# Interleaving the groups at a change of pass, in a Strassen-Winograd feed-forward stage

## The chip, the cores and the metric

The kernel runs on one core of one Trainium2 chip. The metric is the device time of one execution in microseconds (us), as the median of the runs. An engine works through its own queue of instructions in order; TensorE (PE) multiplies, VectorE (DVE) and ScalarE (ACT) work element by element, GpSimd (POOL) does a few sums, SyncE (SP) issues the DMAs.

## What is computed

One layer of a hybrid decoder on 512 positions of width 2048, in float32. The part that matters here is the last one, the convolutional GLU, with 5632 hidden channels:

```
h = rms_norm(x, norm2_w)
u = causal_dwconv(h @ w_up, ffn_conv_w, ffn_conv_b)   # w_up: 2048 x 11264, conv over 3 positions
u_gate, u_val = jnp.split(u, 2, axis=-1)
return x + (jax.nn.silu(u_gate) * u_val) @ w_down     # w_down: 5632 x 2048
```

Ahead of it stand the combined input projection, the attention heads, the state-space heads and the output projection.

## The kernel before

Both large products of the feed-forward stage are done by the Strassen-Winograd scheme: a block product of 2 x 2 blocks takes seven block products, P1 to P7, and no longer eight. Each product multiplies a sum of weight blocks by a sum of activation blocks; the latter is called a *kind*. There are seven kinds, one for each product: P5 uses KT1, P1 K11, P6 KT2, P2 K21, P7 KT3, P3 K22, P4 KT4. To keep float32 accuracy on fp32r matmuls, every operand is split into a high part (an ACT copy to fp32r) and a low part (a DVE subtraction), and a product is high x high, high x low and low x high: 24 matmuls of 128 x 256 where there are 8 blocks of contraction, 21 where there are 7.

A *group* is one set of seven products. There are 44 groups of the up stage (0 to 43; NF is 44), one for each 128 gate and 128 value channels, and then three *passes* of the down stage over 7, 8 and 7 blocks of hidden channels (PASSES), eight groups each: 44 to 51, 52 to 59, 60 to 67. In the text, 43.P7 is product P7 of group 43. Within the up stage the kinds stay; every pass has kinds of its own, made from what the up stage stored in DRAM (gd). b_load reads half a kind into a buffer ld (three deep in the first transition, five later), b_split makes its high part on ACT (L1151) and its low part on DVE (L1152) into the tile cmb of this kind. A kind's tile is one buffer, so that the next pass's version can be written only after the last product that uses the old one. That change of kinds is called a transition here.

A product accumulates in a tile x (one PSUM bank, two halves of 256 columns, two buffers) or y (P2). After a product its half is read out: up_after copies P1, P6 and P5 to cP tiles on ACT (L1241) and adds P2, P7, P3 and P4 on DVE (L1243 to L1249); down_after copies or adds into acc (L1219 on ACT, L1221 on DVE). After P4 of an up group follows its tail on DVE: the norm factor, two convolutions, the gate (up_side, L1259 to L1282) and, every second group, sums of the result (L890 to L893).

All order is by hand. The list items holds the products as TensorE takes them, pos the place of each. For product number k the function step_slot(k) issues: what events holds for k (weight loads, some sums), the low part of operand k+2 (split_lo, L1103), what after holds for k (sums s1 and s3, tails, kind splits), the high part of operand k+3 (split, L1094). Weight sums are s1, s2 and s4 on DVE (L1073, L1076 and L1081, L1083) and s3 on POOL (L1069). Weight loads come from SP (L1062), with four buffers rawa and two rawb.

The order of the products before is that of one loop, the same for all groups: a group's P5, P1, P6, P2, P7 with the P3 and P4 of the group ahead between them.

```
for gi in range(1, len(groups) + 1):
    for d, x in ((0, "P5"), (1, "P3"), (0, "P1"), (1, "P4"), (0, "P6"), (0, "P2"), (0, "P7")):
        put(gi - d, x)
```

Of the kernel before, what the change touches and what calls it, by code (L numbers as in the profile page):

```python
# [33 lines left out]
NF = FF // 128  # L34
# [153 lines left out]
def body(ctx, tc, xT, wi, wz, wo, wu, wd0, wd1, wd2, pp, pf, outT, dbg={}):  # L188
# [99 lines left out]
    def pc(name, i=0, n=1):  # L288
        o = _PC[name] + i
        return (p2["par"] if name[0] == "f" else par)[:, o:o + n]  # L290
# [511 lines left out]
    for half in range(2):  # L802
        box = {}
# [154 lines left out]
    for i in range(4, NK):  # L958
        box = {}
# [65 lines left out]
    def side_tile(pool, shape, name, bufs=1):  # L1025
        return pool.tile([128] + shape, F32, name=name, bufs=bufs)


    groups = []
# [10 lines left out]
    items, pos = [], {}  # L1040

    def put(gi, *names):
        for x in names:
            if 0 <= gi < len(groups):
                pos[gi, x] = len(items)
                items.append((gi, x))

    put(0, "P1", "P5", "P2", "P6", "P7")
    for gi in range(1, len(groups) + 1):
        for d, x in ((0, "P5"), (1, "P3"), (0, "P1"), (1, "P4"), (0, "P6"), (0, "P2"), (0, "P7")):  # L1050
            put(gi - d, x)


    raw, chain, parts = {}, {0: pre_op["s"]}, {0: pre_op["P1"]}
    cols = lambda gi: groups[gi]["n"] * 128
# [31 lines left out]
    def split(k):  # L1087
        if k >= len(items):
            return
        gi, x = items[k]  # L1090
        n = cols(gi)
        src = raw[gi, SOURCE[x]] if x in SOURCE else chain[gi]
        h = lp.tile([128, 1024], F32R, name="hi2", bufs=3)
        se.activation(h[:, :n], src[:, :n], AF.Copy)  # L1094
        parts[k] = (h, src)
# [11 lines left out]
    events, after = {}, {}  # L1107

    def at(slot, fn, *args, where=events):
        where.setdefault(slot, []).append(lambda: fn(*args))  # L1110

    for gi in range(len(groups)):
        p5, p1 = pos[gi, "P5"], pos[gi, "P1"]
        p6 = pos[gi, "P6"]
        at(pos[gi, "P4"] - 6, load, gi, "22b")
        if gi:
            at(p5 - 8, load, gi, "21"), at(p5 - 8, load, gi, "22")
            at(p1 - 7, load, gi, "11"), at(pos[gi, "P2"] - 7, load, gi, "12")
        if gi:
            at(p5 - 3 if gi > 1 else 1, add, gi, "s1", where=after)  # L1120
            at(p5 - 3 if gi > 1 else 7, add, gi, "s3", where=after)
        else:
            at(0, add, gi, "s3", where=after)
        at(max(p5 - 1, p6 - 4) if gi else -1, add, gi, "s2"), at(pos[gi, "P3"] - 3, add, gi, "s4")
# [35 lines left out]

    for p in range(len(PASSES)):
        g0 = NF + 8 * p
        base = pos[g0 - 1, "P5"]
        slots = [2, 4, 5, 7, 8, 9, 9, 10, 11, 11, 12, 13, 14, 15]
        k0 = len(b_list)
        b_list += [(p, t, h) for t in (KT1, K11, KT2, K21, KT3, K22, KT4) for h in range(2)]
        early = 5
        for q in range(14):
            at(base + slots[q], b_split, k0 + q, where=after)
        for q in range(14):  # L1170
            at(base - 6 + q // 2 if q < early else base + slots[q - (5 if p else 3)] + 1, b_load, k0 + q)
        if p == 0:
            at(base + 36, down_pool, where=after)

    def twin(kinds, n):

# [29 lines left out]
    box = {}  # L1206
# [29 lines left out]
    def up_after(g, x):  # L1236
        X, i = g["X"], g["i"]
        ug, uv = box["ug%d" % (i % 2)], box["uv%d" % (i % 2)]
        if x in ("P1", "P6", "P5"):
            g[x] = side_tile(box["pool"], [256], "c" + x, 2 if x == "P5" else 1)  # L1240
            se.activation(g[x], X[:, 256:] if x == "P5" else X[:, :256], AF.Copy)  # L1241
        elif x == "P2":
            ve.tensor_tensor(ug[:, 2:258], g["Y"][:, :256], g["P1"], op=OP.add)  # L1243
        elif x == "P7":
            ve.tensor_tensor(uv[:, 258:514], X[:, :256], g["P5"], op=OP.add)
        elif x == "P3":
            ve.tensor_tensor(ug[:, 258:514], X[:, 256:], g["P6"], op=OP.add)
        else:
            ve.tensor_tensor(uv[:, 2:258], X[:, :256], rbc[:, :256], op=OP.mult)  # L1249
            up_side(i, ug, uv)  # L1250

    def up_side(i, ug, uv):
        pool = box["pool"]
        tt = {}

        def conv(u, ci, name, n):
            if n == 0:
                tt[name] = side_tile(pool, [S], name)
                se.activation(tt[name], u[:, 2:514], AF.Identity, bias=pc("fcb", ci), scale=pc("fcw", ci * 3 + 2))  # L1259
            ve.scalar_tensor_tensor(tt[name], u[:, n:n + S], pc("fcw", ci * 3 + n), tt[name],  # L1260
                                    op0=OP.mult, op1=OP.add)

        def val0():
            conv(uv, NF + i, "tv", 0)
            se.activation(tt["tg"], tt["tg"], AF.Silu)

        def last():
            if i % 2 == 0:
                box["gt"] = side_tile(pool, [8, 256], "gt")
            o = 2 * (i % 2)  # L1270
            ve.tensor_tensor(box["gt"][:, o:o + 2, :].rearrange("p a b -> p (a b)"), tt["tg"], tt["tv"], op=OP.mult)

        def t_sums(n):
            sums(ve, box["gt"], n)
            if n:
                pr = i // 2
                p = max(q for q in range(3) if PASSES[q][0] <= pr)
                at(t0 + (11 if i < NF - 1 else 10), sy.dma_start, gd[p][:, pr - PASSES[p][0]], box["gt"])

        t0 = pos[i, "P4"] + (15 if i >= NF - 2 else 0)  # L1280
        for d, fn in ((0, lambda: ve.tensor_tensor(ug[:, 2:514], ug[:, 2:514], rbc, op=OP.mult)),
                      (1, lambda: ve.tensor_tensor(uv[:, 258:514], uv[:, 258:514], rbc[:, 256:], op=OP.mult)),  # L1282
                      (3, lambda: conv(ug, i, "tg", 0)), (4, lambda: conv(ug, i, "tg", 1)), (5, val0),
                      (6, lambda: conv(uv, NF + i, "tv", 1)), (6, last)):
            at(t0 + d, fn, where=after)
        if i % 2:
            at(t0 + 7, t_sums, 0, where=after), at(t0 + (10 if i < NF - 1 else 8), t_sums, 1, where=after)
# [13 lines left out]
    for gi, g in enumerate(groups):  # L1301
        if g["ph"] == "down":
            p5 = pos[gi, "P5"]
# [20 lines left out]
    def run(slot, where=events):  # L1324
        for fn in where.pop(slot, ()):
            fn()

    def step_slot(slot):
        run(slot)
        if slot > 1:  # L1330
            split_lo(slot + 2)
        run(slot, after)
        if slot > 0:
            split(slot + 3)

    for n in range(2):
# [22 lines left out]
    split_lo(3)  # L1359
    next(last)  # L1360
    at(2, lambda: list(last), where=after)
    for k, (gi, x) in enumerate(items):
        g = groups[gi]
        if x == "P5" and gi or k == 0:
            g["X"] = box["ps"].tile([128, 512], F32, name="x")
        if x == "P2":
            g["Y"] = box["ps"].tile([128, 512], F32, name="y")
        out = g["Y"][:, :256] if x == "P2" else g["X"][:, 256:] if x in ("P5", "P3") else g["X"][:, :256]
        h, l = parts.pop(k)
        bk = g["kinds"][KIND[x]]  # L1370
        n = g["n"]
        fresh = x in ("P5", "P2") if k > 1 else k == 0
        if x == "P3" and (gi in (1, 2, 4, 15, 30) or gi >= NF and g["m"] in (1, 2, 4)):
            tw = box["twin"]
            for a, b, last in ((h, bk[:, 1], False), (h, tw, False), (l, tw, True)):
                for q in range(n):
                    pe.matmul(out, a[:, q * 128:(q + 1) * 128], b[:, q, :], start=False,  # L1377
                              stop=last and q == n - 1, skip_group_check=True)
            (up_after if g["ph"] == "up" else down_after)(g, x)
            step_slot(k)  # L1380
            continue
        for part in ((range(n - 1), range(n - 1, n)) if k < 4 else (range(n),)):
            for q in part:
                w = h[:, q * 128:(q + 1) * 128]
                pe.matmul(out, w, bk[:, 0, q, :], start=fresh and q == 0, stop=False, skip_group_check=True)  # L1385
                pe.matmul(out, w, bk[:, 1, q, :], start=False, stop=False, skip_group_check=True)  # L1386
            for q in part:
                pe.matmul(out, l[:, q * 128:(q + 1) * 128], bk[:, 0, q, :], start=False, stop=q == n - 1,  # L1388
                          skip_group_check=True)
        if k == 0:  # L1390
            continue
        if k == 1:
            start_up()
            up_after(g, "P1")
            step_slot(0)
        (up_after if g["ph"] == "up" else down_after)(g, x)
        step_slot(k)
    for slot in sorted(events):
        run(slot)
# [21 lines left out]
```

## Time and profile before

| | us |
|---|---|
| median of 3 runs (2064.23 to 2066.41) | 2065.65 |
| the profiled execution | 2066.1 |
| its span, first to last instruction | 2064.1 |
| TensorE busy | 2041.0 |
| VectorE busy | 1556.5 |
| ScalarE busy | 1018.4 |

The feed-forward stage begins at about 780 us in the span. The up stage runs to about 1617, the three passes follow. Lines of the profile name the tile written and the tiles read (out<-in), then shape, count, busy time and, in brackets, the idle time ahead of the instruction with what ended it.

### The profile page before, as it was taken

Reading aid. Unit: us, or ns where it says so; the run is one execution under the profiler, and the core shown is the slowest. Engines: PE = TensorE matmul, PEld = TensorE weight load, DVE = VectorE, ACT = ScalarE, POOL = GpSimd, SP = SyncE. Lnnn points to the kernel's source line nnn. Section 1 sums busy time; section 2 is a strip of 40 time slices with the busy share of each in tenths; the row PEclk is TensorE's granted clock in tenths of the full one; section 3 lists DMA queues with packets and bytes.
Section 4 is the critical chain, followed back from the end, with each engine's and each line's share of the span. In section 5 each row is a group of like instructions: output and inputs, shape, how many; then the busy total and the mean of one; then the engine's idle time right before and its main releaser. Section 6 shows DMA issues by size and latency. Waiting matters only on the chain.

```text
span 2064.1 us, 37659 instructions
## 1 busy us (share of the span) xinstructions
PE 2041.0 (99%) x15366; PEld 1929.7 (93%) x15366; DVE 1556.5 (75%) x2185; ACT 1018.4 (49%) x1513; POOL 221.9 (11%) x127
## 2 busy tenths in 40 slices
PE   9999999999999999999999999999999999999999
PEld 8889888888888889999999999999999899999999
DVE  6535555345565558999999999999999987967876
ACT  6433435344444446555555555555555654644643
POOL 0020000000000001101110110111111111211210
PEclk9999999999999999999999999999999999999999
DMA  5232222332224546445445444444446667856873
GB/s 196 79 109 92 82 72 72 102 103 83 82 72 134 177 160 227 158 149 195 154 152 186 164 160 168 174 164 158 171 177 205 217 187 213 263 154 206 256 227 122
DMA packets 111228, 320.84 MB, mean 155 GB/s; under 512 B 10384, under 2 KB 34768, under 8 KB 108240
## 3 DMA queue, kind: packets, MB, share of 16 engines
q1 hardware_dynamic: 108320, 308.48, 44.2%
q0 software_dynamic: 2736, 9.96, 3.0%
q8 instruction: 120, 1.97, 0.4%
q14 instruction: 52, 0.43, 0.1%
HBM read 276.43 MB, written 43.55 MB: 155 GB/s over the span
## 4 chain that ended last, share of the span: by engine, by line
PE 94%; DVE 3%; DMA 1%; issue 1%; ACT 1%; SPq 0%; POOL 0%; DVEq 0%; ACTq 0%; POOLq 0%
PE acc L183 31%; PE x L1386 16%; PE x L1388 16%; PE x L1385 16%; PE sm L183 4%; PE y L1386 3%; PE y L1388 3%; PE y L1385 3%; PE x L1377 2%; DVE cmb L1152 1%; DVE lo L1103 1%; DMA ld<-gd 0%; DMA rawa<-wu 0%; DVE lo L183 0%; DMA raw<-wi 0%
## 5 line engine op out<-in xcount | busy, mean ns | idle before, releaser
L1386 PE MATMUL x<-cmb,hi 128*128 128x256 f32 x3054 | 715.7, 277 | 8.6 <-DVE cmb L1152 8.6
L1385 PE MATMUL x<-cmb,hi 128*128 128x256 f32 x3054 | 715.2, 277 | 2.8 <-ACT cP L1241 1.5
L1386 PEld LDWEIGHTS x<-cmb,hi 128*128 128x128 f32 x3054 | 574.1, 188 | 10.7 <-DVE cmb L1152 10.5
L1385 PEld LDWEIGHTS x<-cmb,hi 128*128 128x128 f32 x3054 | 574.1, 188 | 3.6 <-issue 1.8
L1388 PE MATMUL x<-cmb,lo 128*128 128x256 f32 x3054 | 411.9, 277 | 0.3 <-DVE lo L1103 0.3
L1388 PEld LDWEIGHTS x<-cmb,lo 128*128 128x128 f32 x3054 | 376.8, 188 | 0.5 <-DVE lo L1103 0.5
L183 DVE TENSOR_TENSOR lo<-raw,hi 128x512 fp32r<-128x512 f32 (+1 forms) x240 | 164.4, 691 | 229.1 <-ACT hi L183 212.3
L1094 ACT ACTIVATE hi<-s 128x1024 fp32r<-128x1024 f32 (+1 forms) x201 | 200.9, 1000 | 214.4 <-DVE s L1073 142.9
L183 PE MATMUL acc<-A,hi 128*128 128x512 f32 x704 | 279.2, 397 | 0.9 <-ACT hi L183 0.9
L183 PE MATMUL acc<-A,lo 128*128 128x512 f32 x704 | 275.5, 391 | 0.0
L183 PE MATMUL acc<-B,hi 128*128 128x512 f32 x704 | 274.9, 390 | 0.0
L183 ACT ACTIVATE hi<-raw 128x512 fp32r<-128x512 f32 (+1 forms) x240 | 150.0, 629 | 238.2 <-PE acc L183 202.0
L1103 DVE TENSOR_TENSOR lo<-s,hi 128x1024 fp32r<-128x1024 f32 (+1 forms) x201 | 238.3, 1186 | 29.1 <-issue 26.0
L1069 POOL TENSOR_TENSOR rawb<-rawa,rawb 128x1024 f32<-128x1024 f32 (+1 forms) x67 | 166.4, 2484 | 833.7 <-DVE s L1073 816.2
L1103 DVE TENSOR_TENSOR lo<-rawa,hi 128x1024 fp32r<-128x1024 f32 (+1 forms) x203 | 240.4, 1184 | 18.7 <-PE x L1388 12.8
L1094 ACT ACTIVATE hi<-rawa 128x1024 fp32r<-128x1024 f32 (+1 forms) x203 | 208.5, 1027 | 12.1 <-PE x L1386 10.5
L183 PEld LDWEIGHTS acc<-A,lo 128*128 128x128 f32 x704 | 132.5, 188 | 28.7 <-DVE lo L183 0.6
L183 PEld LDWEIGHTS acc<-A,hi 128*128 128x128 f32 x704 | 132.9, 189 | 27.0 <-ACT hi L183 1.2
L183 PEld LDWEIGHTS acc<-B,hi 128*128 128x128 f32 x704 | 132.8, 189 | 26.1
L1241 ACT ACTIVATE cP<-x 128x256 f32<-128x256 f32 x132 | 50.6, 384 | 197.7 <-PE x L1388 197.7
L183 PE MATMUL acc<-hi,A 128*128 128x256 f32 (+2 forms) x448 | 134.6, 300 | 0.7 <-DVE u L183 0.7
L183 PE MATMUL acc<-hi,B 128*128 128x256 f32 (+2 forms) x448 | 132.7, 296 | 0.0
(236 smaller groups left out, 2895.2 us busy)
## 6 DMA issues: line engine op xcount, KB each, us to landing
rawa<-wu SPq DMA_DIRECT2D x175, 512.0 KB, 3.6
raw<-wi SPq DMA_DIRECT2D x79, 512.0 KB, 3.6
rawa<-wd SPq DMA_DIRECT2D x64, 448.0 KB, 4.3
rawb<-wu SPq DMA_DIRECT2D x44, 512.0 KB, 4.5
gd<-gt SPq DMA_DIRECT2D x22, 1024.0 KB, 4.4
raw<-wo SPq DMA_DIRECT2D x32, 512.0 KB, 3.6
rawa<-wd SPq DMA_DIRECT2D x32, 512.0 KB, 4.3
ld<-gd SPq DMA_DIRECT2D x27, 512.0 KB, 6.9
```

The lines of the kernel that those rows point to most:

```text
L183: return fn(out, *args, **kw)
L1069: (po if gi else ve).tensor_tensor(r, raw[gi, "11"][:, :n], r, op=OP.subtract)
L1094: se.activation(h[:, :n], src[:, :n], AF.Copy)
L1103: ve.tensor_tensor(l[:, :n], src[:, :n], h[:, :n].bitcast(F32), op=OP.subtract)
L1152: ve.tensor_tensor(lo, ld[:, :m, :], hi.bitcast(F32), op=OP.subtract)
L1241: se.activation(g[x], X[:, 256:] if x == "P5" else X[:, :256], AF.Copy)
L1377: pe.matmul(out, a[:, q * 128:(q + 1) * 128], b[:, q, :], start=False, stop=last and q == n - 1, skip_group_check=True)
L1385: pe.matmul(out, w, bk[:, 0, q, :], start=fresh and q == 0, stop=False, skip_group_check=True)
L1386: pe.matmul(out, w, bk[:, 1, q, :], start=False, stop=False, skip_group_check=True)
L1388: pe.matmul(out, l[:, q * 128:(q + 1) * 128], bk[:, 0, q, :], start=False, stop=q == n - 1, skip_group_check=True)
```

## The change

For six pairs of groups, (42, 43), (44, 45), (50, 51), (52, 53), (58, 59) and (60, 61), the products are put in pairs. The second group's product follows the first group's of the same name from P2 on, and in the pairs behind a transition from P5 on. In the pairs ahead of a transition, the P3 and P4 of the group before are still to be done; they go between the first group's P5, P1 and P6, and the second group's P5, P1 and P6 follow in a row. A group that stands behind two pairs (46, 54, 62) has no older P3 and P4 left to put between its own products. The 14 half kinds of a pass are split at slots 7 to 25, counted from the P5 of the last pair, where they were split at slots 2 to 15, counted from the P5 of the last group. The weight loads near the transitions are called two products later. The tails of groups 42 and 43 start 15 and 21 products after their P4. Ahead of the up stage's second group, the high part of operand 5 goes behind the read-out of 0.P6 on ACT. cP1 and cP6 have two buffers.

```diff
+    PAIRS = {NF - 2, NF, NF + 6, NF + 8, NF + 14, NF + 16}
     put(0, "P1", "P5", "P2", "P6", "P7")
-    for gi in range(1, len(groups) + 1):
-        for d, x in ((0, "P5"), (1, "P3"), (0, "P1"), (1, "P4"), (0, "P6"), (0, "P2"), (0, "P7")):
-            put(gi - d, x)
-
+    gi, open_ = 1, 0
+    while gi < len(groups):
+        c, d = gi, gi + 1
+        if gi not in PAIRS:
+            put(c, "P5")
+            if open_ is not None:
+                put(open_, "P3")
+            put(c, "P1")
+            if open_ is not None:
+                put(open_, "P4")
+            put(c, "P6", "P2", "P7")
+            open_ = c
+            gi += 1
+            continue
+        if open_ is None:
+            put(c, "P5"), put(d, "P5"), put(c, "P1"), put(d, "P1"), put(c, "P6"), put(d, "P6")
+        else:
+            put(c, "P5"), put(open_, "P3"), put(c, "P1"), put(open_, "P4"), put(c, "P6")
+            put(d, "P5", "P1", "P6")
+        for x in ("P2", "P7", "P3", "P4"):
+            put(c, x), put(d, x)
+        open_ = None
+        gi += 2
+    put(open_, "P3", "P4")
+    near = set()
+    for c in PAIRS:
+        near |= {c, c + 1} if c < NF or c % 8 != NF % 8 else {c, c + 1, c + 2, c + 3}
...
-        if gi:
+        if gi in near:
+            at(p5 - 6, load, gi, "21"), at(p5 - 6, load, gi, "22")
+            at(p1 - 5, load, gi, "11"), at(pos[gi, "P2"] - 6, load, gi, "12")
+        elif gi:
             at(p5 - 8, load, gi, "21"), at(p5 - 8, load, gi, "22")
             at(p1 - 7, load, gi, "11"), at(pos[gi, "P2"] - 7, load, gi, "12")
...
-            at(p5 - 3 if gi > 1 else 7, add, gi, "s3", where=after)
+            at(max(p5 - 3, pos[gi, "P7"] - 9) if gi > 1 else 7, add, gi, "s3", where=after)
...
-        base = pos[g0 - 1, "P5"]
-        slots = [2, 4, 5, 7, 8, 9, 9, 10, 11, 11, 12, 13, 14, 15]
+        base = pos[g0 - 2, "P5"]
+        slots = [7, 8, 10, 11, 12, 14, 15, 16, 18, 19, 21, 22, 24, 25]
...
-            at(base - 6 + q // 2 if q < early else base + slots[q - (5 if p else 3)] + 1, b_load, k0 + q)
+            at(base - 1 + q // 2 if q < early else base + slots[q - (5 if p else 3)] + 1, b_load, k0 + q)
         if p == 0:
-            at(base + 36, down_pool, where=after)
+            at(base + 47, down_pool, where=after)
...
-            g[x] = side_tile(box["pool"], [256], "c" + x, 2 if x == "P5" else 1)
+            g[x] = side_tile(box["pool"], [256], "c" + x, 2)
...
-        t0 = pos[i, "P4"] + (15 if i >= NF - 2 else 0)
+        t0 = pos[i, "P4"] + {NF - 2: 15, NF - 1: 21}.get(i, 0)
...
-        if slot > 0:
+        if slot > 0 and slot != 2:
             split(slot + 3)
...
+    events[3].insert(0, lambda: split(5))
```

On TensorE, before, where 43.P5 (tile x_17307) ends and the next product begins; lo is the low part of a weight operand, the names behind the arrow are kind and operand:

```order
L1386 MATMUL x_17307<-cmb0_5981,hi2_17236 128x256
L1388 MATMUL x_17307<-cmb0_5981,lo2_17267 128x256 [waits DVE_49]
L1388 MATMUL x_17307<-cmb0_5981,lo2_17267 128x256 x7
L1385 MATMUL x_17060<-cmb5_7267,hi2_17269 128x256 [waits DVE_49,Activation_49]
L1386 MATMUL x_17060<-cmb5_7267,hi2_17269 128x256
```

The same place in the changed kernel, where 43.P5 (now x_17239) ends:

```order
L1414 MATMUL x_17239<-cmb0_5981,hi2_17173 128x256
L1416 MATMUL x_17239<-cmb0_5981,lo2_17202 128x256 [waits DVE_49]
L1416 MATMUL x_17239<-cmb0_5981,lo2_17202 128x256 x7
L1413 MATMUL x_17239<-cmb2_5983,hi2_17205 128x256 [waits Activation_49]
L1414 MATMUL x_17239<-cmb2_5983,hi2_17205 128x256
```

Before, 42.P3 in another tile followed; now 43.P1 follows in the same tile, and its first matmul waits for ACT. On ACT the read-outs of 43 that were two products apart (cP5_17332, cP1_17397 before) now follow each other with one high part between them, and the kind splits (cmb0) come after them. Before:

```order
L1241 ACTIVATE cP5_17332<-x_17307 128x256
L1094 ACTIVATE hi2_17338<-rawa_17228 128x1024
L1259 ACTIVATE tv_17367<-uv1_7187,par2_7085 128x512
L1265 ACTIVATE tg_17302<-tg_17302 128x512
L1094 ACTIVATE hi2_17371<-s_17232 128x1024
L1241 ACTIVATE cP1_17397<-x_17307 128x256
L1151 ACTIVATE cmb0_17403<-acc_s_17119 128x1024
```

In the changed kernel:

```order
L1268 ACTIVATE cP5_17264<-x_17239 128x256
L1118 ACTIVATE hi2_17268<-rawa_17163 128x1024
L1268 ACTIVATE cP1_17294<-x_17239 128x256
L1286 ACTIVATE tg_17298<-ug1_7185,par2_7085 128x512
L1118 ACTIVATE hi2_17301<-rawa_17200 128x1024
L1268 ACTIVATE cP6_17327<-x_17239 128x256
L1178 ACTIVATE cmb0_17331<-acc_s_17048 128x1024
```

Three read-outs stand here where two stood, with the first kind split behind the third of them. On DVE, from the read-out of 43.P2 (y) to that of 43.P7 (uv1 from x), before:

```order
L1243 TENSOR_TENSOR ug1_7185<-y_17477,cP1_17397 128x256
L1083 TENSOR_TENSOR s_17232<-rawa_17265,s_17232 128x1024
L1103 TENSOR_TENSOR lo2_17506<-s_17470,hi2_17475 128x896
L1152 TENSOR_TENSOR cmb2_17508<-ld_17159,cmb2_17508 128x1024
L1245 TENSOR_TENSOR uv1_7187<-x_17307,cP5_17332 128x256
```

In the changed kernel:

```order
L1270 TENSOR_TENSOR ug1_7185<-y_17375,cP1_17294 128x256
L1107 TENSOR_TENSOR s_16983<-rawa_17163,s_16983 128x1024
L1127 TENSOR_TENSOR lo2_17404<-rawb_17044,hi2_17373 128x1024
L1287 SCALAR_TENSOR_TENSOR tv_17369<-uv1_7187,par2_7085,tv_17369 128x512
L1298 TENSOR_TENSOR gt_17171<-tg_17298,tv_17369 128x512
L1272 TENSOR_TENSOR uv0_7183<-x_17061,cP5_17086 128x256
L1107 TENSOR_TENSOR s_17167<-rawa_17200,s_17167 128x1024
L1127 TENSOR_TENSOR lo2_17440<-s_16983,hi2_17408 128x1024
L1179 TENSOR_TENSOR cmb2_17442<-ld_17089,cmb2_17442 128x1024
L890 TENSOR_TENSOR gt_17171<-gt_17171 128x512
L1272 TENSOR_TENSOR uv1_7187<-x_17239,cP5_17264 128x256
```

Between the two read-outs there is one more product, 42.P7, whose read-out (uv0) stands among the rows, a second sum and low part, and the end of group 41's tail. Four more instructions of this walk stand ahead of the first row: the read-out of 42.P2, a low part, half of kind 0 (768 columns) and a convolution step.

## The prediction, made blind

> **What bounds the kernel now.** I read the page's busy table first, then the stages by windows, then who waited for whom on TensorE. The table says TensorE all the way, VectorE (DVE) next.
>
> ```profile
> PE 2041.0 (99%) x15366; PEld 1929.7 (93%) x15366; DVE 1556.5 (75%) x2185; ACT 1018.4 (49%) x1513; POOL 221.9 (11%) x127
> ```
>
> A busy TensorE hides lost time, because one matmul lasts longer than the step from one to the next. So I count matmuls in windows. The columns are length, then busy time and (count) for each engine, the granted clock, and DMA.
>
> ```profile
> core 0: us, PE busy (x) PEld busy (x) DVE busy (x) ACT busy (x) POOL busy (x), PEclk, DMA share, GB/s
> 823.00:1600.00 777.00, 777.00 (x6854) 777.00 (x6854) 736.29 (x918) 411.17 (x531) 100.83 (x41) 1.00 0.48 169
> 1600.00:1670.00 70.00, 65.46 (x547) 64.60 (x547) 63.51 (x74) 43.66 (x59) 9.31 (x5) 0.98 0.62 200
> 1670.00:1755.00 85.00, 85.00 (x751) 85.00 (x750) 65.92 (x79) 41.45 (x60) 16.46 (x11) 1.00 0.72 210
> 1755.00:1812.00 57.00, 54.09 (x457) 52.81 (x456) 50.68 (x51) 37.17 (x45) 11.80 (x5) 1.00 0.81 252
> 1922.00:1956.00 34.00, 31.96 (x276) 31.37 (x276) 31.70 (x36) 23.36 (x31) 7.74 (x4) 1.00 0.83 247
> ```
>
> The up stage steps at 777/6854 = 0.11336 us per matmul: 24 make a product of 2.72 us, 21 one of 2.38. Between the transitions nothing is lost (751 × 0.11336 = 85.1 of 85). The three stretches with a change of kinds lose 70 − 547 × 0.11336 = **8.0**, 57 − 51.8 = **5.2** and 34 − 31.3 = **2.7 us**. That is all this change can win there: **15.9 us**. DVE is busy 95% of the up stage (736.29 of 777), so it can take little more ahead of the first transition.
>
> Who is waited for there:
>
> ```profile
> PE x L1386 <- DVE cmb L1152: 8.6, 10, 1.6
> PE x L1385 <- ACT cP L1241: 1.5, 1, 1.5
> PE x L1385 <- DVE acc L1221: 1.2, 2, 0.6
> ...
> 1624.39 4.04 DMA ld<-gd
> 1630.81 5.10 DMA ld<-gd
> ```
>
> The first row is the late kinds (cmb, written by the splits in L1152). The last two, from the chain of waits, show the loads in front of the splits: before, a load is issued about one product ahead of its split and lands 4 to 5 us later.
>
> **Part 1: the kinds are no longer late.** By the changed order both halves of the first kind are split by 42.P2 (group 42, product P2), eight products before 44.P5 uses it; the last kind is ready three products, 3 × 2.38 = 7.1 us, before 44.P4. The tails of groups 42 and 43 go under the first pass, where DVE is 65.92 of 85 us busy; the third pass alone reads what they store. So the 15.9 us fall away as waits on cmb. What is late next are two other things.
>
> **Part 2: handovers inside one tile, added.** In a pair that has an older group's P3 and P4 before it, the second group runs P5, P1, P6 back to back in one accumulator tile x; the single group behind each run of pairs (46, 54, 62) does so too. That makes 2 × 6 = 12 places where a product's first matmul waits for the read-out of the product just ahead of it; before, a foreign product stood between. The trace has this case at its end, where the last group runs P7, P3, P4 in one tile:
>
> ```profile
> 2051.80 0.28 PE L1385 MATMUL x<-cmb,hi 128*128 128x256 f32 x1
> 2054.95 0.36 PE L1385 MATMUL x<-cmb,hi 128*128 128x256 f32 x1 [0.61 <-DVE acc L1221]
> 2058.21 0.36 PE L1385 MATMUL x<-cmb,hi 128*128 128x256 f32 x1 [0.61 <-DVE acc L1221]
> 2054.38 0.42 DVE L1221 TENSOR_TENSOR acc<-x,acc 128x256 f32<-128x256 f32 x1 [0.96 <-PE x L1388]
> 1591.88 1.07 PE L1388 MATMUL x<-cmb,lo 128*128 128x256 f32 x8
> 1592.99 0.38 ACT L1241 ACTIVATE cP<-x 128x256 f32<-128x256 f32 x1 [2.52 <-PE x L1388]
> ```
>
> The starts lie 3.15 and 3.26 us apart where 2.38 is the step: a handover costs 0.77 and 0.88 us, though P3 writes the other half of the tile. There DVE reads out; at the twelve new places it is ScalarE (ACT), 0.38 instead of 0.42 us, started 0.04 us after the matmuls end (1591.88 + 1.07 = 1592.95). I take **0.75 each, 9.0 us**; bounds 0.64 (the ACT copy with its drain, 0.17 + 0.04 + 0.38 + 0.05) and 0.88, so 7.7 to 10.6. Nothing covers it: TensorE takes its products in order, so all later ones stand behind the waiting matmul. [...]
>
> **Part 3: DVE's lag.** DVE still has the same 14 splits in each transition, now beside 23 products and no longer beside 14. Durations, from one start to the next:
>
> ```profile
> 1595.71 0.42 DVE L1243 TENSOR_TENSOR ug<-y,cP 128x256 f32<-128x256 f32 x1
> 1596.05 1.22 DVE L1083 TENSOR_TENSOR s<-rawa,s 128x1024 f32<-128x1024 f32 x1
> 1597.18 1.22 DVE L1103 TENSOR_TENSOR lo<-s,hi 128x1024 fp32r<-128x1024 f32 x1
> 1599.90 0.74 DVE L1260 SCALAR_TENSOR_TENSOR tg<-ug,par,tg 128x512 f32<-128x512 f32 x1
> 1600.56 1.22 DVE L1081 TENSOR_TENSOR s<-s,rawa 128x1024 f32<-128x1024 f32 x1
> 1609.88 0.69 DVE L1271 TENSOR_TENSOR gt<-tg,tv 128x512 f32<-128x512 f32 x1
> 1610.49 0.42 DVE L1249 TENSOR_TENSOR uv<-x,rbc 128x256 f32<-128x256 f32 x1
> 1632.03 0.95 DVE L1152 TENSOR_TENSOR cmb<-ld,cmb 128x768 fp32r<-128x768 f32 x1
> 1632.90 1.08 DVE L1103 TENSOR_TENSOR lo<-rawb,hi 128x896 fp32r<-128x896 f32 x1
> 1633.90 1.09 DVE L1073 TENSOR_TENSOR s<-rawb,rawa 128x896 f32<-128x896 f32 x1
> ```
>
> So 256 columns cost 0.34, 512 0.61, a convolution step 0.66, 768 0.87, 896 1.00, 1024 1.13 us. In the changed order DVE reads 42.P2 out, and until it reads 43.P7 out has 14 instructions: 0.34 + 1.13 + 0.87 + 0.66, then 0.34 + 1.13 + 1.13 + 0.66 + 0.61, then 0.34 + 3 × 1.13 + 0.61 = 11.2 us. TensorE's three products in that time take 8.16, so DVE is 3.1 us late. 43.P3 must wait for that read-out (the same tile); between them is 42.P3 alone, 2.72 us. Stall: 3.1 + 0.8 − 2.72 = **1.2 us**. From there to the read-out of 43.P4 DVE has four read-outs (1.36), three low parts of 1.13 and one of 1.00, three splits (2.87), two sums of 1.00 and two of 0.34, 11.3 us, beside four products of 2.72, 10.9, so it is 3.1 + 0.4 − 1.2 = 2.3 late, and 45.P5, which takes over that tile, has 44.P5's 2.38 as cover: 2.3 + 0.8 − 2.38 = **0.7 us**. For low parts of operands that come late meanwhile I add 0.5: 2.4 us in the first transition (0.5 to 4, as the lag of 3.1 is a quarter less or more).
>
> In the second transition the up tails are gone but the next groups' sums are 1024 wide: from 50.P2's read-out to the sum for 52.P5 DVE has six read-outs (2.04), six low parts (6.0), two sums (2.0), four splits (4.5) and that sum (1.13), 15.7 us, beside five products, 11.9: 3.8 late. ACT, which splits that sum (1.0) and then reads 50.P4 out (0.4), is 0.5 late for 52.P5; with the following P5 and P1 I take 1.7 (0.5 to 2.5). In the third, from 58.P7 to 60.P5, DVE has four read-outs (1.36), seven low parts (7.52), six splits (6.0) and four sums (4.13), 19.0 us, beside 18.7 of seven products: 0.5 (0 to 1). Sum **4.6 us** (1 to 7.5).
>
> **Part 4: the start.** One split (operand 5) goes behind the read-out cP6 on ACT.
>
> ```profile
> 791.01 1.02 ACT L1094 ACTIVATE hi<-s 128x1024 fp32r<-128x1024 f32 x1 [1.40 <-DVE s L1073]
> 791.93 0.38 ACT L1241 ACTIVATE cP<-x 128x256 f32<-128x256 f32 x1
> 800.47 2.88 DVE L1196 TENSOR_TENSOR cmb<-ld,cmb 128x1024 fp32r<-128x1024 f32 x1 [0.29 <-ACT cmb L1195]
> 803.28 1.21 DVE L1103 TENSOR_TENSOR lo<-rawa,hi 128x1024 fp32r<-128x1024 f32 x1
> ```
>
> cP6 no longer stands behind 0.9 us of that split (791.01 to 791.93), so 0.P7 can start that much sooner. But DVE runs without a break into the low part at 803.28, and that releases 1.P1 whatever came before; its one gap is 0.29 us. I take −0.3 (bounds −0.9 and +0.4, the split's wait behind a copy of 0.38).
>
> The weights of the groups at the transitions are asked for two products later than before, so that their first reader, the sum s1 on DVE, stands three products behind the call (7.1 to 8.2 us) and no longer five. The slowest landing around the second transition is
>
> ```profile
> rawb<-wd SPq DMA_DIRECT2D x3, 512.0 KB, 7.9
> ```
>
> so at worst 7.9 − 7.1 = 0.8 us of DVE's time there, which the bounds of that transition hold. SP waits for no product, only for a free buffer, and so mostly calls sooner; I add nothing. The second buffers of cP1 and cP6 only remove waits.
>
> **Sum.** Before 15.9 lost, after 9.0 + 4.6 = 13.6: −2.3; with the start −2.6. The profiled execution took 2066.1 (span 2064.1 and 2.0 around it), 0.45 above the median of 2065.65. So 2066.1 − 2.6 = 2063.5 there, and **2063.0** for the median. A measurement of this kernel can tell about 0.2%, 4.1 us, from no change: under 2061.5 is faster, over 2069.8 slower.
>
> **Rivals.**
>
> *Handovers cheap, lag hidden.* If each handover costs its lower bound (7.7) and DVE's lag 1.5, 9.2 us remain of 15.9: −6.7 − 0.3, **2058.7**. For it: ACT is 49% busy and ready, and the lag sum rests on a few tenths per product. Against it: the 0.77 and 0.88 measured. Chance 0.25.
>
> *Loads late in a three-deep ring, slower.* In the first transition a split's load goes into the buffer that the third split before it frees, three products (7.5 us) ahead, less DVE's lag of 3.1: 4.4 us remain. Median landing of ld<-gd around the first transition (1590 to 1660) and the second (1750 to 1810):
>
> ```profile
> ld<-gd SPq DMA_DIRECT2D x4, 512.0 KB, 4.1
> ld<-gd SPq DMA_DIRECT2D x9, 512.0 KB, 7.0
> ```
>
> At 4.1 it just holds. At 7.0 every turn of the ring is 2.6 us short; ACT stands at the split with read-outs and high parts queued behind it. Three turns make +7.8 against the forecast: **2070.8**. It decides from a landing of about 4.4 us. For it: weight loads queue behind these loads on SP. Against: kinds then still have several products of reserve, and 0.62 DMA share leaves room. Chance 0.08.
>
> *The pitch drops.* After the longest stall of the first transition the matmuls step slower:
>
> ```profile
> 1636.00:1642.00 6.00, 4.23 (x22) 4.03 (x23) 5.31 (x6) 4.29 (x5) 2.08 (x1) 0.73 0.85 268
> 1642.00:1662.00 20.00, 20.00 (x171) 20.00 (x171) 17.43 (x22) 11.87 (x16) 3.52 (x2) 0.99 0.69 205
> 2056.00:2061.00 5.00, 4.24 (x36) 3.88 (x34) 0.54 (x2) 0.00 (x0) 0.00 (x0) 1.00 0.16 59
> ```
>
> 20/171 = 0.1170, 3% over 0.11336. If many short stalls did the same over three stretches of 70 us, that is +6.7: **2069.7**. Against it: in the last row, between two handovers, the granted clock stays 1.00. [...] Chance 0.07.
>
> That the change doesn't do what it says I give nothing: the order shows the kinds ahead of their use.
>
> **How the numbers follow.** Forecast 0.60, own range 2060.5 to 2066.5 (half of the way to the bounds of the terms 9.0, 4.6 and 0.3, all on one side). Range for 8 in 10: down to the cheap case, 2058.7, up between forecast and slower rivals, **2058.5 to 2068.0**. Faster: 0.22 of the cheap case and 0.08 of the forecast's low end, 0.30. Slower: 0.06 of the ring, 0.03 of the pitch, 0.01 more, 0.10. Same: 0.60.
>
> **What would show it.** Waits on cmb near 0 in the three transitions; twelve waits of about 0.6 us of TensorE on ACT's cP, acc_s, ld and acc read-outs; a few waits on DVE's ug and uv and lo around 43.P3 and 45.P5. Wrong if those twelve starts lie 2.4 or 2.7 us apart (Part 2), if waits on lo or cmb of over 5 us are left in one transition (Part 3), or if ACT waits for ld.

## The result and the profile after

| | us |
|---|---|
| before, median of 6 runs | 2065.55 (2063.65 to 2066.66) |
| after, median of 6 runs | 2081.8 (2078.33 to 2082.84) |
| ratio | 1.0077, 95% interval 1.0064 to 1.009 |
| the profiled execution of after, its span | 2082.84, 2081.1 |

The change costs 16 us; 2063.0 was forecast, in a range up to 2068.0. On the page of after, DVE's busy time moved although no work was added:

```profile
PE 2046.3 (98%) x15366; PEld 1933.0 (93%) x15366; DVE 1568.7 (75%) x2185; ACT 1017.5 (49%) x1513; POOL 215.3 (10%) x127
```

DVE was 1556.5 us busy with the same 2185 instructions; now it is 12.2 us longer. So some of them last longer than they did. In the stretches with a change of kinds, matmuls were counted again (the second and third windows are longer than those of before, since the transitions are):

```profile
1600.00:1670.00 70.00, 65.80 (x561) 64.41 (x560) 63.42 (x74) 41.81 (x54) 8.90 (x5) 1.00 0.63 198
1755.00:1822.00 67.00, 60.86 (x515) 60.06 (x514) 59.53 (x56) 38.14 (x46) 10.59 (x7) 0.97 0.77 239
1922.00:1976.00 54.00, 49.81 (x412) 49.61 (x412) 48.24 (x49) 31.33 (x42) 9.68 (x7) 0.94 0.70 211
```

By 0.11336 us for each matmul they lose 6.4, 8.6 and 7.3 us, where 8.0, 5.2 and 2.7 had been lost. These windows leave out what is lost ahead of them, 2.5 us just before 1600 alone; a count by product that takes it in stands under the experiments. Whom TensorE waits for, from 780 us on (engine, tile and line, the one waited for, us in all, times, longest):

```profile
PE x L1416 <- DVE lo L1127: 10.2, 4, 4.4
PE x L1413 <- ACT acc L1246: 5.0, 10, 0.7
PE x L1413 <- ACT cP L1268: 3.2, 3, 2.3
PE x L1413 <- DVE uv L1276: 1.7, 1, 1.7
```

The waits on cmb are gone, the handovers are there (ACT's acc and cP), and there is a new one: 10.2 us on the low parts of operands, two of over 4 us. The timeline shows where the larger comes from (start, duration, engine, line, operation, tiles):

```profile
1773.79 1.23 DVE L1127 TENSOR_TENSOR lo<-s,hi 128x1024 fp32r<-128x1024 f32 x1
1775.01 6.16 DVE L1179 TENSOR_TENSOR cmb<-ld,cmb 128x1024 fp32r<-128x1024 f32 x1
1781.09 1.22 DVE L1105 TENSOR_TENSOR s<-s,rawa 128x1024 f32<-128x1024 f32 x1
...
1774.45 0.88 POOL L1257 DMA_DIRECT2D x2d<-acc  x1 [2.71 <-ACT acc L1246]
1775.02 5.06 POOL L1093 TENSOR_TENSOR rawb<-rawa,rawb 128x1024 f32<-128x1024 f32 x2
...
1783.49 2.08 PE L1416 MATMUL x<-cmb,lo 128*128 128x256 f32 x8 [4.43 <-DVE lo L1127]
```

A split of a kind, 1.22 us elsewhere, lasts 6.16 us. Beside it GpSimd (POOL) runs the sums s3 of groups 52 and 53 back to back, 5.06 us, and the split ends 1.09 us after them, about its own duration. GpSimd had them together because s1 of the two groups now stand one product apart, and both sums stood behind the store of 51.P4. Everything on DVE is late from there, and TensorE waits 4.43 us in 52.P1. The third transition has the same:

```profile
1936.64 5.59 DVE L1179 TENSOR_TENSOR cmb<-ld,cmb 128x1024 fp32r<-128x1024 f32 x1
...
1936.63 4.51 POOL L1093 TENSOR_TENSOR rawb<-rawa,rawb 128x896 f32<-128x896 f32 x2
```

In the first, three operations last 2.54, 2.22 and 1.82 us in place of 0.69, 1.09 and 1.22, each beside one sum. The middle one and its sum:

```profile
1629.58 2.22 DVE L1097 TENSOR_TENSOR s<-rawb,rawa 128x896 f32<-128x896 f32 x1
...
1628.72 2.13 POOL L1093 TENSOR_TENSOR rawb<-rawa,rawb 128x896 f32<-128x896 f32 x1 [32.85 <-DVE uv L1276]
```

The trace of before has GpSimd's sums too, and there little harm is seen: in the transitions one DVE operation stands, 2.08 us for 0.95 at 1636.81. Two places show why:

```profile
1838.16 0.42 DVE L1221 TENSOR_TENSOR acc<-y,acc 128x256 f32<-128x256 f32 x1 [0.29 <-PE y L1388]
1838.51 1.22 DVE L1083 TENSOR_TENSOR s<-rawa,s 128x1024 f32<-128x1024 f32 x1
1839.63 1.22 DVE L1103 TENSOR_TENSOR lo<-s,hi 128x1024 fp32r<-128x1024 f32 x1
...
1838.01 2.40 POOL L1069 TENSOR_TENSOR rawb<-rawa,rawb 128x1024 f32<-128x1024 f32 x1 [3.61 <-DVE s L1073]
...
1777.13 2.35 DVE L1152 TENSOR_TENSOR cmb<-ld,cmb 128x1024 fp32r<-128x1024 f32 x2
...
1777.37 4.38 POOL L1069 TENSOR_TENSOR rawb<-rawa,rawb 128x1024 f32<-128x1024 f32 x1 [3.68 <-DVE s L1073]
```

At 1838 the sum takes its 2.40 us and the three DVE operations beside it their usual time. Each of the three reads one operand from PSUM: s, x and y are tiles there (chain[gi] comes from the pool box["ps"]). At 1777 two splits, which read ld and cmb from SBUF, had begun first, and it is the sum that lasts 4.38 us: it waits for both (to 1779.40) and then takes 2.4. In the order of before, the read-out of P2, the sum s4 and a low part of s followed s1, so between 823 us and the end no sum and no DVE operation stood outside the transitions (the sums last 2.40 to 2.46 us there, 2.12 to 2.14 with 896 columns); where a sum met splits in a transition, it was mostly the sum that waited (six last 2.72 to 4.38 us), and nothing waited for it. The changed order put splits of kinds beside the sums, and there DVE waits.

So **theory 1**: a DVE operation with both inputs in SBUF and a sum of GpSimd exclude each other, and the one that comes second stands until the other has ended; an operation that reads an operand from PSUM runs beside the sum. The rows at 1775 (6.16 us for 1.22 beside the sums) and 1838 (0.42, 1.22 and 1.22 us, the sum 2.40) agree; that it holds beyond such rows was the author's guess, and the experiments are there to try it. Where an operation writes to does not decide it in these rows: s<-rawb,rawa writes PSUM and stands (2.22 us for 1.09 at 1629.58, in after), lo<-s,hi writes SBUF and does not (1.22 us at 1839.63). **Theory 2**: DVE is late by its own work, and GpSimd only happens to run there. **Theory 3**: the handovers cost it all.

### The profile page after: what moved, and what is told of

Its sections match the earlier page's. It is cut to its first block, busy times and chain, and to the rows that moved or that the text cites. A ratio compares the mean times of both kernels' runs of the same rounds, so it can differ in the third digit from the quotient of the medians.

```text
span 2081.1 us, 37661 instructions
## 1 busy us (share of the span) xinstructions
PE 2046.3 (98%) x15366; PEld 1933.0 (93%) x15366; DVE 1568.7 (75%) x2185; ACT 1017.5 (49%) x1513; POOL 215.3 (10%) x127
## 4 chain that ended last, share of the span: by engine, by line
PE 91%; DVE 4%; issue 2%; DMA 2%; ACT 1%; SPq 0%; POOL 0%; DVEq 0%; ACTq 0%; POOLq 0%
PE acc L183 30%; PE x L1416 16%; PE x L1413 16%; PE x L1414 15%; PE sm L183 4%; PE y L1413 3%; PE y L1414 3%; PE y L1416 3%; PE x L1405 2%; DVE lo L1127 1%; DVE cmb L1179 1%; DMA gd<-gt 0%; DVE lo L183 0%; DMA rawa<-wu 0%; ACT t L183 0%
## 5 line engine op out<-in xcount | busy, mean ns | idle before, releaser
L1416 PE MATMUL x<-cmb,lo 128*128 128x256 f32 x3054 | 414.1, 277 | 10.4 <-DVE lo L1127 10.2
L1093 POOL TENSOR_TENSOR rawb<-rawa,rawb 128x1024 f32<-128x1024 f32 (+1 forms) x67 | 160.8, 2411 | 934.3 <-DVE s L1097 866.3
L1118 ACT ACTIVATE hi<-rawa 128x1024 fp32r<-128x1024 f32 (+1 forms) x203 | 208.6, 1028 | 12.7 <-PE x L1414 10.5
```

The source lines that it names most:

```text
L1093: (po if gi else ve).tensor_tensor(r, raw[gi, "11"][:, :n], r, op=OP.subtract)
```

## The experiments

The column "lost" is worked out from TensorE's timeline: from each product's start to the next, less 2.72 us (2.38 with seven blocks), summed over the products 290 to 334, 346 to 391 and 402 to 449, the three transitions.

| kernel | median us | ratio to before, 95% interval | lost in the three transitions, us |
|---|---|---|---|
| before | | | 8.3, 5.6, 3.2 |
| after | 2081.8 | 1.0077 (1.0064, 1.009) | 10.5, 11.3, 10.6 |
| e1, near sums on DVE | 2076.3 | 1.0052 (1.0035, 1.0069) | 13.2, 8.8, 5.9 |
| e2, new order in the pairs | 2076.4 | 1.0053 (1.0038, 1.0068) | 8.3, 10.0, 9.0 |
| e4, both | 2074.1 | 1.0044 (1.0029, 1.0059) | 12.4, 9.0, 4.6 |
| e3, before with late sums | 2081.0 | 1.0075 (1.0055, 1.0095) | |
| e5, after, no near sums | 2065.7 | 1.0005 (0.9996, 1.0014) | 6.5, 5.7, 4.8 |
| e6, before, no near sums | 2064.8 | 0.9996 (0.9986, 1.0005) | 7.7, 5.6, 3.2 |
| e7, e2, no near sums | 2063.2 | 0.9988 (0.9979, 0.9997) | 5.5, 4.8, 3.1 |
| b1, sums placed | 2104.1 | 1.0189 (1.0175, 1.0203) | |
| b2, mended | 2063.0 | 0.9993 (0.9984, 1.0002) | 7.0, 4.2, 3.1 |
| b3, twin later | 2058.9 | 0.9966 (0.9954, 0.9978) | 5.0, 3.3, 2.2 |

### The sums on the other engine, and the handovers

e1 changes one line of after:

```diff
-            (po if gi else ve).tensor_tensor(r, raw[gi, "11"][:, :n], r, op=OP.subtract)
+            (po if gi and gi not in near else ve).tensor_tensor(r, raw[gi, "11"][:, :n], r, op=OP.subtract)
```

> The changed kernel with the sums s3 of the groups near a transition on VectorE (DVE) instead of GpSimd. Theory 1 (block): a DVE operation whose two inputs both lie in SBUF stands still while GpSimd's sum runs (5.06 us at 1775.02, 4.51 us at 1936.63); then the 5.6 and 5.3 us lost at 52.P1 and 60.P1, 2.0 at 61.P1 and 1.7 of the 2.5 at 43.P1 go, and no DVE operation lasts over 1.3 us there; the 14 sums cost DVE 1.0 to 1.13 us each, of which part shows: 2068 to 2078, most likely 2072. Theory 2 (lag: DVE simply has too much to do in the transitions): 14 us more work on DVE makes it slower, 2084 to 2096, and the long waits on lo stay. Theory 3 (handovers cost all of it): no change, 2082.

No DVE operation of the transitions lasts over 1.3 us any more, and the second and third lose 2.5 and 4.7 us less, with more work on DVE. Theory 2 falls: it wanted the time to go up. The first loses 2.7 us more: in the up stage DVE is 95% busy, the sums of 42 and 43 come on top, and DVE stands 1.16 us for the weights of the second; TensorE loses 2.3 us behind 42.P6.

e2 changes the order inside the pairs:

```diff
         if open_ is None:
+            e = gi + 2
             put(c, "P5"), put(d, "P5"), put(c, "P1"), put(d, "P1"), put(c, "P6"), put(d, "P6")
+            put(c, "P2", "P7"), put(d, "P2"), put(c, "P3"), put(d, "P7"), put(c, "P4"), put(d, "P3")
+            put(e, "P5"), put(d, "P4"), put(e, "P1", "P2", "P6", "P7")
...
-            put(d, "P5", "P1", "P6")
-        for x in ("P2", "P7", "P3", "P4"):
-            put(c, x), put(d, x)
...
+        put(d, "P5"), put(c, "P2"), put(d, "P1"), put(c, "P7"), put(d, "P6", "P2", "P7")
+        put(c, "P3"), put(d, "P3"), put(c, "P4"), put(d, "P4")
```

> The changed kernel with another order inside the pairs, so that of the 12 handovers inside one tile 3 are left (P6 to P7 of groups 46, 54, 62); GpSimd's sums stay. Theory 1 (block): 9 handovers of 0.7 us go, the long DVE operations stay wherever a sum of GpSimd meets an operation with both inputs in SBUF, though at other places: 2071 to 2079, most likely 2075. Theory 3 (handovers cost all): about 2065 or less. Theory 2 (lag): last kinds are used two products sooner and DVE has less time, 2078 to 2088.

5.4 us less. The twelve handovers cost 10.3 us in after, the three that are left cost 1.7 each, since ACT reads P6 out behind a high part: 5.2 us of difference, and the rest of the loss stays, so theory 3 falls too. The long operations stay, at other places: with the sums of 52 and 53 apart, each blocks by itself.

```profile
1764.50 3.83 DVE L1101 TENSOR_TENSOR s<-rawb,rawa 128x1024 f32<-128x1024 f32 x1
1770.69 3.85 DVE L1183 TENSOR_TENSOR cmb<-ld,cmb 128x1024 fp32r<-128x1024 f32 x1
...
1764.52 2.70 POOL L1097 TENSOR_TENSOR rawb<-rawa,rawb 128x1024 f32<-128x1024 f32 x1
1770.76 2.69 POOL L1097 TENSOR_TENSOR rawb<-rawa,rawb 128x1024 f32<-128x1024 f32 x1
```

> Both edits together: the new order inside the pairs and the sums of the near groups on VectorE. Theory 1: the gains add up, 2062 to 2071, most likely 2066. Theory 2: the slowest of the three, 2085 to 2100. Theory 3: as the new order alone, about 2065.

A miss: the gains did not add up. 42.P6 now loses 4.4 us and 51.P5 2.4, and most of this is not DVE's work. A sum on DVE has to wait for its weights in DVE's queue, and everything behind it waits too:

```profile
1592.76 1.23 DVE L1097 TENSOR_TENSOR rawb<-rawa,rawb 128x1024 f32<-128x1024 f32 x1 [3.24 <-DMA rawa<-wu]
...
1742.69 1.09 DVE L1097 TENSOR_TENSOR rawb<-rawa,rawb 128x896 f32<-128x896 f32 x1 [4.12 <-DMA rawa<-wd]
```

DVE stands 9.9 us for such loads in e4 and 2.2 in e1. In after, between 1580 and 2000 us, GpSimd waits 21.6 us for rawa<-wd ahead of two sums, and DVE waits for no load.

### The same block made in the kernel before

e3 takes before and lets the sum of 20 groups wait, with no work added on DVE:

```diff
         if name == "s3":
             r = raw[gi, "21"][:, :n]
+            if 10 <= gi < 30:
+                for _ in range(4):
+                    po.memset(used[gi], 0.0)
...
         if name == "s1":
+            used[gi] = raw[gi, "22"]
```

> The kernel before the change, with four fills of 128x1024 ahead of GpSimd's sum s3 in 20 groups of the up stage (10 to 29), each waiting for s1: the sum starts some 4 us later in DVE's order, where the convolution steps and the sums of gt read both inputs from SBUF; before, it ran beside a sum and a low part that read s from PSUM. DVE's own work is unchanged. Theory 1 (block, and only for operations with both inputs in SBUF): in each of these groups a DVE operation lasts 1 to 2.4 us longer; DVE is 95% busy there and has 1 us per group to spare, so 5 to 28 us slower, 2070 to 2094. Rival (a block only where DVE had run empty, whatever it reads): DVE runs without a gap there, so no long operations and no change, 2064 to 2067.

15.6 us slower. In all 20 groups one DVE operation with two SBUF inputs now lasts 2.06 to 2.72 us; there had been none. One of them, a convolution step of 0.74 us:

```profile
989.78 1.21 DVE L1108 TENSOR_TENSOR lo<-s,hi 128x1024 fp32r<-128x1024 f32 x1
990.91 2.72 DVE L1265 SCALAR_TENSOR_TENSOR tg<-ug,par,tg 128x512 f32<-128x512 f32 x1
...
986.71 4.00 POOL L1072 MEMSET rawa<- 128x1024 f32 x4 [13.44 <-DVE s L1078]
990.68 2.40 POOL L1073 TENSOR_TENSOR rawb<-rawa,rawb 128x1024 f32<-128x1024 f32 x1
```

It follows its forerunner without a gap, so a DVE that has run empty is not needed. The fills themselves ran beside readers of PSUM, but for 0.2 us each, so they tell nothing.

### The sums taken away

e5 is after, e6 before and e7 e2's kernel, each with

```diff
         if name == "s3":
+            if gi in near:
+                return
```

(in e6 the same groups by number). These three kernels leave 18 sums out and so do not compute the layer; they are for timing alone.

> The changed kernel with the sums s3 of groups 42 to 47, 50 to 55 and 58 to 63 left out on every engine: P7 there takes row 21 itself as its operand, so neither GpSimd nor DVE has that work, and the rest of the order stays. Theory 1 (block): the long DVE operations of the transitions (2.54, 2.22, 1.82, 6.16 and 5.59 us) go and nothing comes for them: 52.P1 and 60.P1 each lose about 1 us and no longer 5.6 and 5.3, 61.P1 0.6 for 2.0, 43.P5 0.8 for 2.5, and about 1 us more in the first transition; 13 us in all: 2065 to 2072, most likely 2068.5. Theory 2 (lag, DVE has too much of its own work and GpSimd doesn't matter): DVE's work is unchanged, so 2079 to 2082.

> The kernel before the change with the sums of the same groups left out (P7 takes row 21 itself). There GpSimd's sums ran beside sums and low parts that read s from PSUM; one DVE operation stood, 2.08 us in place of 0.95 at 1636.81. Theory 1: at most that 1.1 us goes, 2063.5 to 2065.5. If the sums cost DVE time wherever they stand, as much as in the changed kernel, 2050 to 2055.

> The new order inside the pairs with the same sums left out. Theory 1: the order alone has long DVE operations of 2.6, 2.2, 1.8, 2.2, 3.8, 3.9, 1.9, 3.6 and 3.6 us; without them 10 to 12 us less than its 2076.4: 2062 to 2068, most likely 2065. With the first of these runs it tells what the handovers cost when nothing blocks: 9 of them, 0.7 each, 6 us less than that run, less what ACT and DVE are late for the P6 to P7 handovers that are left (1.7 each). Theory 2: 2074 to 2077.

This settles it. The same 18 sums weigh 16.1 us in after (2081.8 to 2065.7), 13.2 in e2's order, and 0.4 in before, within what can be told. Without them DVE is 1555.6 us busy in e5, 13.1 less than in after, and the transitions (columns as in the windows above) lose 5.4 us in the first stretch and 3.0 and 2.9 in the others:

```profile
1600.00:1670.00 70.00, 67.28 (x570) 65.88 (x570) 62.62 (x74) 42.95 (x56) 1.95 (x2) 1.00 0.65 202
1755.00:1812.00 57.00, 54.95 (x476) 54.16 (x474) 50.05 (x51) 36.29 (x44) 3.47 (x4) 1.00 0.82 255
1922.00:1966.00 44.00, 42.92 (x363) 42.30 (x362) 36.89 (x40) 29.14 (x41) 3.46 (x4) 1.00 0.79 226
```

By product, 52.P1 lost 5.6 us in after and under 0.3 in e5, 60.P1 5.3 and under 0.3, 61.P1 2.0 and 0.5, 43.P5 2.5 and 0.6, 44.P5 1.9 and 0.5.

### The sums placed

b1 to b3 have e2's order with another handover left in it (P1 to P6 for P6 to P7), keep every sum on GpSimd and start those of nine groups (43, 44, 45, 51, 52, 53, 59, 60, 61) where DVE reads PSUM. DVE writes a token just ahead of such operations, and GpSimd's fill of it, and so the sum behind, waits for that (5.54 us ahead of the fill at 1773.17 in b3):

```diff
+        if name == "s3t":
+            ve.memset(p2["tok"], 0.0)
+            po.memset(p2["tok"], 0.0)
+            name = "s3"
...
+            elif gi in firsts:
+                at(p5 + 1, add, gi, "s3t", where=after)
+            elif gi - 1 in firsts:
+                at(pos[gi - 1, "P3"] - 3, add, gi, "s3t", where=after)
+                at(pos[gi - 1, "P3"] - 3, add, gi - 1, "s4", where=after)
```

(firsts are 44, 52, 60; s2 of the second group goes behind the token of the first.)

> All sums kept, on GpSimd: the new order inside the pairs (with P1 to P6 of groups 46, 54, 62 as the one handover left, in place of P6 to P7), and each sum s3 of the groups that blocked (43, 44, 45, 51, 52, 53, 59, 60, 61) held back by a token, a fill of 128x1 on DVE and then on GpSimd, that DVE writes just ahead of two or three operations that read s or a product from PSUM; s2 and s4 of these groups and four halves of the kinds move by one to three products for it, and the split of operand 5 at the start stands again where it stood before the change. Theory 1: no DVE operation of over 1.6 us in the transitions, though GpSimd does the same sums; the lost time of the kernel without these sums (2063.2), less 3 times 0.9 for the cheaper handover and 0.9 at the start, plus up to 3 for tokens and partly met operations: 2058 to 2064, most likely 2061, below the kernel before. If it is the sums themselves and not what they meet that costs: 2072 to 2077.

A miss by 43 us, mostly for two reasons other than what the sums meet (one DVE operation still stood, 2.07 us for 0.69 at 1621.76). All matmuls of the up stage step more slowly (777/6671 = 0.1165 us, more below), and a store that DVE's gt waits for (7.34 us) stood behind loads asked for too soon:

```profile
823.00:1600.00 777.00, 777.00 (x6671) 777.00 (x6670) 718.19 (x892) 399.19 (x516) 98.23 (x40) 1.00 0.45 160
...
1619.67 0.69 DVE L1324 TENSOR_TENSOR gt<-tg,tv 128x512 f32<-128x512 f32 x1 [7.34 <-DMA gd<-gt]
```

> The kernel with placed sums once more, with three things mended that the run before it showed: its token was a tile of 128x1, four bytes a row, and all tiles allocated behind it moved by four bytes, with matmuls 0.1165 us apart in place of 0.1134 in the whole up stage; the token is now 256 bytes a row. Its loads for groups 42 and 43 were asked for earlier and stood in SP's queue ahead of a store that DVE waited 7.3 us for; they are as in the changed kernel again. And the last two kinds are split one product earlier. The start is as in the changed kernel. Theory 1: matmuls 0.1134 apart again, no DVE operation of over 1.6 us in the second and third transitions, 2058 to 2064, most likely 2061.

> The aligned kernel with placed sums, and the second half of kind K22 split one product later, ahead of the low part there: in the run before it, ScalarE had both halves and the copy twin (1.93 us) ahead of a high part that TensorE then waited for, 0.8 us in each of the three transitions (45.P2, 53.P2, 61.P2). If that is all, 2 us less than its 2063.0: 2059 to 2063, most likely 2061; the loss would have to fall by 2 more for a difference from the kernel before that can be told.

b2 is 18.8 us below after, with the same sums on the same engine. Part of that is the order, since e2 is 5.4 us below after; but e2's order without any of the 18 sums took 2063.2 us (e7), so in b2 the sums cost nothing that can be told. From before b2 can't be told either. Its step is 777/6848 = 0.1135 us again. b3 is 6.7 us faster than before, 0.34% (0.22 to 0.46), the one version with all its sums that is clear of before. Its transitions lose 3.8 us less than b2's, where 2 less was expected. The sum of group 52 in b3, beside operations that read s:

```profile
1773.02 1.23 DVE L1115 TENSOR_TENSOR s<-s,rawa 128x1024 f32<-128x1024 f32 x1
1773.04 0.06 DVE L1098 MEMSET tok<- 128x1 f32 x1
1774.15 2.47 DVE L1137 TENSOR_TENSOR lo<-s,hi 128x1024 fp32r<-128x1024 f32 x2
...
1773.30 2.40 POOL L1103 TENSOR_TENSOR rawb<-rawa,rawb 128x1024 f32<-128x1024 f32 x1
```

Nothing stands: 1.23 and 2.47 for two on DVE, 2.40 on GpSimd. DVE's busy time on the page is 1556.5 us, as in before.

### A tile of four bytes

To see whether the small token alone made b1's matmuls slow, before was given a tile and nothing else:

```diff
+    po.memset(lp.tile([128, 1], F32, name="pad"), 0.0)
```

> The kernel before the change with one more tile of 128x1, four bytes a row, allocated where the token of the placed sums was and filled once; nothing else differs. If the four bytes alone slow the matmuls (operands behind it start four bytes further on), they step 0.1165 us in the up stage in place of 0.1134, 2.7%, over the 1300 us of the second phase 30 to 38 us: 2095 to 2104. If the slower step came from the other edits of that kernel: 2064 to 2067.

> The same with a tile of 128x16, 64 bytes a row. If only a shift that is no multiple of 64 bytes hurts: 2064 to 2067 and a step of 0.1134. If any shift of those tiles hurts, as much as with four bytes.

2098.3 us (ratio 1.0161, 1.0131 to 1.019) and 2111.7 (1.0226, 1.0196 to 1.0255). The up stage of each:

```profile
823.00:1600.00 777.00, 777.00 (x6671) 777.00 (x6669) 718.57 (x893) 399.14 (x516) 98.51 (x40) 1.00 0.45 161
...
823.00:1600.00 777.00, 777.00 (x6591) 777.00 (x6590) 709.19 (x881) 396.03 (x513) 95.83 (x39) 1.00 0.45 159
```

777/6671 = 0.1165 and 777/6591 = 0.1179 us a matmul, at a granted clock of 1.00. Four bytes explain b1's step. 64 bytes are no remedy: neither branch of the expectation held, the step is slower still than with four. 256 bytes (in b2) cost nothing: 0.1135 us.

## Why the prediction was wrong

**Part 1, kinds no longer late: right in the mechanism, the gain somewhat too large.** The waits on cmb, 9.4 us in before, are gone. But the prediction let all 15.9 us go with them, and by product 2.3 us in before lie in products that lose under 0.3 each. Such losses stay: 2.3 us in after, 3.2 in e5.

**Part 2, handovers: right.** Eleven of the twelve cost 0.64 to 0.83 us, where 0.75 was taken. P5 to P1, which write two different halves of the tile, cost 0.64 as well. The twelfth, 43.P5 to P1, cost 2.46, because DVE's operation at 1593.88 stood (2.54 us for 0.69); without the sums it is 0.64. All twelve together cost 8.4 us in e5, for 9.0.

**Part 3, DVE's lag: here it failed.** The step is the list of durations "from one start to the next", 1.13 us for 1024 columns and so on, used for every instruction in the transitions. It takes for granted that an operation lasts as long beside any neighbour. Five in the transitions stood, for 4.9, 4.4, 1.9, 1.1 and 0.6 us, 12.9 in all, and what followed made 16 us of it. Without them the term was about right: in e5 the products that the prediction named or their neighbours lost 2.5 us in the first transition (2.4 forecast), 2.3 in the second (1.7) and 0.5 in the third (0.5). The 3.2 us of small losses named under Part 1 were in no term. e5 came to 2065.7, inside the range.

**What was overlooked.** The change moved s3 (the diff shows it) and the prediction gave that move no cost, though GpSimd's queue belongs to what a moved step passes. And the clue stood among its own rows: the split at 800.47 lasts 2.88 us for 1.22. It was quoted in Part 4 for its gap; asking what ran beside it would have given GpSimd's sum from 799.88 to 802.27, and the split's end 1.08 us behind it. With that, the two pairs of sums that the order puts side by side, 5.06 and 4.51 us as measured, could have been priced.

**Part 4, the start: the size right, the reason half.** As forecast, 0.P7 starts sooner: TensorE loses 0.7 us behind 0.P6 and no longer 1.8. But 1.6 us are lost behind 1.P1 for 0.8 before, since the split there lasts 3.26 us for 2.88, beside the same sum of GpSimd (in b1 it lasts 1.73, and 0.2 us are lost). Together 0.P6 to 1.P1 lose 3.9 us for 4.2, −0.2 for the −0.3 forecast, and that can't be told from nothing: the traces of e3 and e6, which start as before does, have 3.8 and 4.4.

**The rivals.** Handovers cheap: no. Loads late: no wait of ACT for ld. The pitch drops: steps right behind the long waits are slow (0.21 to 0.22 us for 0.113 from 1785.36 on, behind the wait of 4.43; the granted clock is 0.97 and 0.94 in the windows of the result), but as a follower of the blocks; in e5 it is 1.00. None had GpSimd in it.

## What to carry to other kernels

When an order changes on an engine, look at what then runs beside GpSimd. Here a sum there cost nothing that can be told next to DVE operations that read PSUM (1.22 us for the low part at 1839.63 in before; b2 took 2063.0 us, e2's order without the 18 sums 2063.2), and up to its whole length next to those that read both inputs from SBUF (4.9 us longer at 1775.01 in after, beside two sums of 5.06 us together). To move the sums to DVE was no remedy by itself: in e4 DVE stands 9.9 us for their loads, in the queue that others need. The split that lasted 6.16 us, where the median of its line is 1.22, was a wait that the views of waits did not show; look for such ones by the minimum, median and maximum of a form, or by an engine's busy time that grows while its count of instructions does not (1568.7 us for 1556.5, with 2185 both times). Where both had to run, a token of 0.06 us put the sum at the right place in b3, in a tile whose size left the matmul step as it was (256 bytes a row, 0.1135 us in b2).

## What the runs showed of the hardware

- In three places with two in a row, the side that held on kept on: two sums of GpSimd held one DVE operation for both (6.16 us at 1775.01 and 5.59 at 1936.64, after), and two DVE operations held a sum for both (4.38 us at 1777.37, before). The one that waited got no turn in between. The recorded starts did not always tell which of two goes first: in e2 a split recorded from 1770.69 stood (3.85 us for 1.22) for a sum recorded from 1770.76.
- A small tile allocated ahead of others changed the matmul step: 0.1134 us as the kernel is, 0.1165 with four bytes a row, 0.1179 with 64, 0.1135 with 256 (in b2), all at a granted clock of 1.00. By what way was not shown: that it is where the tiles behind it start is the author's inference from the order of allocation, and which operand is concerned was not tried.
